# The second part of an output projection: another order of its features, two blocks interleaved, and four weight sets of the next stage prepared in it

## The chip, the cores and the metric

The kernel runs on one core of a Trainium2 chip. The metric is the device time of one execution in microseconds (us); the time of before is the median of three runs.

## The reference

One layer of a streaming encoder, for 256 new frames and 64 frames of a running stream, together 320 positions, with 2048 features:

```
h = RMSNorm(x);  p = h @ w_in
A = conformer convolution of 1024 channels (width 31, group norm, swish)
B = gated DeltaNet, 8 heads of 128
x = x + RMSNorm(concat(A, B) @ w_out)          # the output projection
h = RMSNorm(x);  gu = causal depthwise conv (width 3) of h @ w_up
x = x + RMSNorm((silu(gate) * up) @ w_down)
```

Outputs are the two results and the new states. All is float32.

## The kernel before

**Layout and arithmetic.** Activations lie with 128 features on the partitions and the 320 positions along the free dimension, so the 2048 features are 16 tiles. Every weight and every activation is split into a high part (fp32r) and a remainder, and each product is three matmuls: high by high, high by remainder, remainder by high. A weight set is loaded by SyncE's queue into a staging tile `w` (pool `wst`, three buffers, L207), ScalarE converts it to the high part `whi` (L214), and VectorE takes the remainder `wlo` (L215); both lie in pool `wsp`, three buffers each. A staging buffer is free again when its remainder is taken, a `wsp` buffer when the last matmul has read it. `load_split` does all three. `block_matmul` (L222 on) runs a whole block so and calls `tick` after every matmul, which lets background jobs (the convolution's and DeltaNet's later steps) put their instructions in at chosen points.

**The output projection** has 16 output blocks and 16 feature tiles, in the order `KORDER` (0 to 7 from the convolution, 8 to 15 from the heads). Its first part (L995 to L1000) takes the first 11 features of blocks 0 to 14, with weights `w_out1` in sets of 6 and 5 features, and copies each sum from PSUM to a tile `m[n]` (L1000). Then `while jobs` (L1001) puts out what is left of the jobs; at this point that is the last step of the convolution's channel group 7: transposes (L592), the swish `af` (L594), and the split of feature 7 into `bh` (L238) and `bl` (L239). The second part (L1037 to L1063) goes over the blocks again, with the last five features and one set `w_out2[n]` of 128 x 640 each: 15 matmuls a block (L1052 to L1054). Its PSUM tiles come from pools `ps_p` (blocks 0 and 1, then 4 and 5, and so on) and `ps_t`, two buffers each. After a block VectorE adds the sum to `m[n]` (L1060), ScalarE squares it (L1020, L1023), VectorE sums the squares (L1025), and ScalarE scales `m[n]` (L1063). Block 15 does its first part here too, as 6 and 5 features and then the five. In the same loop the residual `x1` is loaded (L1041), in 16 pieces of 160 KB, and behind blocks 4 and 8 one set each of the up projection, 128 x 1024, is loaded and split into pool `ug`, which has two buffers.

**The stage behind it** (L1064 to L1110): the norm's factor (`rstd`, `rstd_rows`, with idle matmuls that keep TensorE busy), then for each feature tile k: scale (L1084), add the residual (L1085), high part (L1089) and remainder (L1090). For odd k up to 11 the up sets 2 to 7 are loaded and split here, through the common pools. For k = 1, 3 and 5 their VectorE work is queued behind the remainder of the tile before and their ScalarE work behind the last scaling of `m`. `up_group` then runs four blocks of the up projection side by side, 12 matmuls per feature (L1108). Behind it the squares of `x1` are summed for the next norm.

**Order.** Instructions of an engine run in the order in which a scheduler puts them, by priority (`tc.high_priority`) and by when it expects them to be ready. `tc.issue_after(ins)` queues what a block of code puts on the engine of `ins` behind `ins`, and only on that engine.

Of the kernel before, what the change touches and what calls it, by code (L numbers as in the profile page):

```python
# [9 lines left out]
F32 = mybir.dt.float32  # L10
F32R = mybir.dt.float32r
AF = mybir.ActivationFunctionType
ALU = mybir.AluOpType
# [4 lines left out]
P = 128  # L18
D = 2048
KB = D // P  # L20
TP = 256
TS = 64
T = TP + TS
# [5 lines left out]
HALF = 1024  # L29
NWARM = 8  # L30
GAP = 20
PRI_J = 1500
LAG_GATE = 60
LAG_CONV = 40
# [33 lines left out]
K1 = 11  # L68
# [3 lines left out]
FIRST_V = 32  # L72
NFIRST = len(FIRST)
FW = NFIRST * P
KORDER = (0, 1, 2, 3, 4, 8, 9, 10, 11, 12, 13, 5, 6, 7, 14, 15)

S_ = 4

# [22 lines left out]
def trunk_kernel(ctx, tc, ins, outs):  # L101
    nc = tc.nc
    V, S, G, PE = nc.vector, nc.scalar, nc.gpsimd, nc.tensor
    PRI_W = 600
    boost = [0]
    PRI_E = 3000
# [19 lines left out]
    def advance(job, behind=None):  # L126
        with tc.issue_after(behind or dense[0]), tc.high_priority(offset=PRI_J):
            try:
                wait, job[2], job[3], *kind = next(job[1])
                job[0] = dense[1] + wait  # L130
                job[4] = kind
            except StopIteration:
                jobs.remove(job)
        return next(i for i in reversed(nc.cur_bb.bb.instructions) if i.engine == dense[0].engine)
# [10 lines left out]
    def newest(engine, n0):  # L145
        return next((i for i in reversed(nc.cur_bb.bb.instructions[n0:]) if i.engine == engine), None)

    def tick(mm):
        dense[0] = mm.ins
        dense[1] += 1  # L150
        if dense[1] % GAP == 0:
            g, t0, behind, due = 0, held_t[0], dense[0], []
# [25 lines left out]
    act = ctx.enter_context(tc.tile_pool(name="act", bufs=1))  # L178
# [10 lines left out]
    def pv(name, a=None, b=None):  # L189
        o, w = PAR[name]  # L190
        if a is None:
            return par[:, o:o + w]
        return par[:, o + a:o + (a + 1 if b is None else b)]
# [8 lines left out]
    def load_dma(src):  # L202
        w = wst.tile([P, HALF], F32, tag="w", name="w")
        dst = w[:, 0:src.free_size()]
        if len(src.shape) == 3:
            dst = dst.rearrange("p (a f) -> p a f", a=src.shape[1])
        nc.sync.dma_start(dst, src)  # L207
        return w

    def split_w(w, width, pool=None):  # L210
        pool = pool or wsp
        hi = pool.tile([P, HALF], F32R, tag="whi", name="whi")
        lo = pool.tile([P, HALF], F32R, tag="wlo", name="wlo")
        S.copy(hi[:, 0:width], w[:, 0:width])  # L214
        V.tensor_tensor(lo[:, 0:width], w[:, 0:width], hi[:, 0:width].bitcast(F32), ALU.subtract)  # L215
        return hi, lo

    def load_split(src, width, pool=None):
        with tc.high_priority(offset=boost[0]):
            return split_w(load_dma(src), width, pool)  # L220
# [51 lines left out]
    def keep_warm(ps, n, after=None):  # L272
        with ExitStack() as e:
            if after is not None:
                e.enter_context(tc.issue_after(after.ins))
            for _ in range(n):
                PE.matmul(ps, wz[:, 0:P], wz, start=True, stop=True)
# [16 lines left out]
    def hx(k):  # L294
        return hi_t[k], lo_t[k]
# [17 lines left out]
    with tc.tile_pool(name="xp", bufs=1) as xp:  # L313
# [25 lines left out]
        with tc.high_priority(offset=PRI_E):  # L339
            keep_warm(psw, NWARM)  # L340

            last = {}
# [42 lines left out]
        for k0 in range(0, KB, 2):  # L385
            hi, lo = pre[k0 // 2]
            for ks in ((k0,), (k0 + 1,)) if k0 < 4 else ((k0, k0 + 1),):
                for wt in (hi, lo):
                    for k in ks:
                        for i, b in enumerate(FIRST):  # L390
                            ps = ready[b][:, 0:T]
                            o = (k - k0) * FW + i * P
                            w = wt[:, o:o + P]
                            xh, xl = hx(k)
# [171 lines left out]
    def conv_tail(b, cvt, left):  # L566
        while left[0]:
            yield GAP, 0, 0
        yield LAG_CONV, 0, 1
# [80 lines left out]
    def gdn_tail(h, st, kq, vT):  # L650
        s = h % NS
        while not gate or (s and "kq" not in st) or (h // NS > 1 and "free" not in sts[h // NS - 2]):
            yield GAP, 1 + 2 * s, 1
        if s == 0:
# [72 lines left out]
    def base_inverse(bt, st):  # L727
# [9 lines left out]
        G.memset(wi_t[:, 0:256:17], 1.0)  # L737
        yield 2 * GAP, 0, 0

        d8, w8 = (t.rearrange("p (b x) -> p b x", b=2)[:, :, 0:128].rearrange("p b (r c) -> p b r c", c=16)[:, :, :, 0:8]  # L740
                  for t in (dn_t, wi_t))
        for r in range(6, -1, -1):
# [5 lines left out]
            if r in (3, 0):  # L748
                yield GAP, 0, 0
        tmp = tmp_t.rearrange("p (r c s) -> p r c s", r=8, c=8)  # L750
# [3 lines left out]
        V.tensor_reduce(x, tmp, AX.X, ALU.add)  # L754
        yield GAP, 0, 0
        V.tensor_tensor(tmp, wi[:, 0:8, 0:8].unsqueeze(2).to_broadcast((nb, 8, 8, 8)),
# [234 lines left out]
    def bx(k):  # L991
        return b_hi[KORDER[k]], b_lo[KORDER[k]]

    m = []
    for n in range(KB - 1):  # L995
        psm = ps_p.tile([P, 512], F32, tag="p", name="psm")
        block_matmul(psm[:, 0:T], ins["w_out1"][n], bx, (6, 5))
        m.append(act.tile([P, T], F32, tag=f"hl{n}", name=f"m{n}"))
        with tc.high_priority(offset=PRI_E):
            S.copy(m[n], psm[:, 0:T])  # L1000
    while jobs:  # L1001
        advance(jobs[0])
    pa.close()
    pb = ctx.enter_context(ExitStack())
    res = pb.enter_context(tc.tile_pool(name="res", bufs=1, reuse_waits="tile"))
# [10 lines left out]
    def square_acc(k, x, whole=False):  # L1016
        nonlocal acc
        if k == 0:
            acc = fb.tile([P, T], F32, tag="acc", name="acc")
            S.activation(acc, x, AF.Square)  # L1020
            return acc
        sq = fb.tile([P, T], F32, tag="sq", name="sq")
        S.activation(sq, x, AF.Square)  # L1023
        if whole or k < KB - 1:
            V.tensor_tensor(acc, acc, sq, ALU.add)  # L1025
        return sq

    ug = tc.tile_pool(name="ug", bufs=2, reuse_waits="tile")
    ugp = ug.__enter__()
    up_src = ins["w_up"][0:4].rearrange("a p f -> p a f")  # L1030

    def up_weights(kk, pool=None):
        return load_split(up_src[:, :, kk * 256:(kk + 1) * 256], HALF, pool)

    upw = []
    nk2 = KB - K1
    for n in range(KB):  # L1037
        hi, lo = load_split(ins["w_out2"][n], nk2 * P)
        if n in (4, 8):
            upw.append(up_weights(len(upw), ugp))  # L1040
        nc.sync.dma_start(x1[:, n:n + 1, :], ins["x"][:, n:n + 1, :])  # L1041
        if n == KB - 1:
            nc.sync.dma_start(fpar, ins["fpar"])
        whole = n == KB - 1
        pool = (ps_p, ps_t)[n // 2 % 2]
        psm = pool.tile([P, 512], F32, tag=pool.name[-1], name="psm2")
        if whole:
            block_matmul(psm[:, 0:T], ins["w_out1"][n], bx, (6, 5), False)
        for j in range(nk2):
            xh, xl = bx(K1 + j)  # L1050
            o = j * P
            PE.matmul(psm[:, 0:T], hi[:, o:o + P], xh, start=(j == 0 and not whole), stop=False)  # L1052
            PE.matmul(psm[:, 0:T], hi[:, o:o + P], xl, start=False, stop=False)
            PE.matmul(psm[:, 0:T], lo[:, o:o + P], xh, start=False, stop=(j == nk2 - 1))  # L1054
        with tc.high_priority(offset=PRI_E):
            if whole:
                m.append(act.tile([P, T], F32, tag=f"hl{n}", name=f"m{n}"))
                src = psm[:, 0:T]
            else:
                V.tensor_tensor(m[n], m[n], psm[:, 0:T], ALU.add)  # L1060
                src = m[n]
            last = square_acc(n, src)
            held = S.activation(m[n], src, AF.Identity, scale=pv("g2", n)).ins  # L1063
    boost[0] = 0  # L1064
    rb2 = act.tile([P, T], F32, tag="rb", name="rb2")
    hi2, lo2 = [], []
    with tc.high_priority(offset=PRI_E):
        psw = ps_p.tile([P, 512], F32, tag="p", name="psw")
        rr, mm = rstd([acc, last])
        keep_warm(psw, 5, mm)  # L1070
        rb1, mm = rstd_rows(rr)
        keep_warm(psw, 10, mm)
        split = None
        for k in range(KB):
            if k % 2 == 1 and k < 13:
                with ExitStack() as e:
                    if k < 7:
                        e.enter_context(tc.issue_after(split))
                        e.enter_context(tc.issue_after(held))
                    upw.append(up_weights(len(upw)))  # L1080
            with ExitStack() as e:
                if 0 < k < 4:
                    e.enter_context(tc.issue_after(added))
                V.tensor_tensor(m[k], m[k], rb1, ALU.mult)  # L1084
            added = V.tensor_tensor(x1[:, k, :], x1[:, k, :], m[k], ALU.add).ins  # L1085
            g = pv("g3", k)
            hi2.append(act.tile([P, T], F32R, tag=f"hh{k}", name=f"hi2_{k}"))
            lo2.append(act.tile([P, T], F32R, tag=f"hl{k}", name=f"lo2_{k}"))
            S.activation(hi2[k], x1[:, k, :], AF.Identity, scale=g)  # L1089
            split = V.scalar_tensor_tensor(lo2[k], x1[:, k, :], g, hi2[k].bitcast(F32), ALU.mult, ALU.subtract).ins  # L1090
# [98 lines left out]
    with tc.high_priority(offset=PRI_E):  # L1189
        last = square_acc(KB - 1, held_y[:, 0:T])  # L1190
# [25 lines left out]
    for step in PLAN_Y.split():  # L1216
        how, ks = step[0], step[1:]
        n = 2 if len(ks) == 4 else 1
        k = int(ks[:len(ks) // n])
# [16 lines left out]
def pack(inputs):  # L1236
# [12 lines left out]
    w_in_t = wtile(w_in[:, :6144], 48)  # L1249
    w_out = wtile(f["w_out"][0].reshape(KB, P, D)[list(KORDER)].reshape(D, D), 16)  # L1250
    par = np.concatenate([
# [63 lines left out]
```

## Time and profile before

| | |
|---|---|
| runs | 1498.56 us median of 3 (1497.97 to 1499.13) |
| profiled execution, from first to last instruction | 1497.8 us |
| PE, DVE, ACT, POOL busy | 99%, 67%, 49%, 15% |
| mean granted TensorE clock | 0.997 |
| DMA | 224.22 MB, mean 150 GB/s |
| first matmul of the second part's block 0 | 500.00 us |
| first matmul of block 15 | 535.98 us |
| first matmul of the up group | 548.88 us |

The page gives the profiled execution's own time as its span; what lies around the span isn't shown by it, and the median of the runs is 0.8 us longer. In the profile PE is TensorE's matmuls, PEld its weight loads, DVE VectorE, ACT ScalarE, POOL GpSimd and SPq the queue of SyncE, which issues the loads. A timeline row gives start and length in us, engine, line, operation, what is written from what, and the count of merged instructions; in brackets the idle time before it and what ended it. The records of successive matmuls overlap, so the distance of their starts is what one costs.

### The profile page before, as it was taken

To read this page: it belongs to the slowest core of one execution; us is meant where nothing else is said; L and a number is where in the kernel's file an instruction comes from. 1 tells how busy PE (TensorE), PEld (TensorE's weight loads), DVE (VectorE), ACT (ScalarE), POOL (GpSimd) and SP (SyncE) were. 2 spreads that over 40 slices of the span, in tenths; PEclk is the share of its full clock that TensorE was granted. 3 is DMA by queue.
4 is the path that set the end of the run, shared out by engine and by line. 5 is a ranking of instruction groups with operands and counts; after the bars stand their busy time and mean duration, and the time that the engine had idled before them with its cause. 6 is when DMAs were issued, how large, how long until landed. Compare 5 with 4: busy or idle time off the path is not lost.

```text
span 1497.8 us, 27263 instructions
## 1 busy us (share of the span) xinstructions
PE 1481.6 (99%) x10609; PEld 1460.4 (98%) x10610; DVE 996.1 (67%) x1816; ACT 727.9 (49%) x1329; POOL 229.2 (15%) x390
## 2 busy tenths in 40 slices
PE   9999999999999999999999999999999999999998
PEld 8999999989999999999999999999999999999997
DVE  6779886978989678766345666445666545666554
ACT  7764556554544565544434444334444333444453
POOL 0111101120010000332002222002223101222101
PEclk9999999999999999999999999999999999999999
DMA  8435453544434744444554444455444455444453
GB/s 289 142 128 157 141 155 120 146 139 134 130 106 142 221 151 141 148 149 128 149 169 151 151 154 134 140 156 164 154 152 141 136 146 173 153 146 152 130 152 118
DMA packets 98281, 224.22 MB, mean 150 GB/s; under 512 B 18792, under 2 KB 39528, under 8 KB 98152
## 3 DMA queue, kind: packets, MB, share of 16 engines
q1 hardware_dynamic: 98008, 222.45, 47.7%
q8 instruction: 83, 1.36, 0.4%
q14 instruction: 46, 0.38, 0.1%
q10 hardware_dynamic: 144, 0.03, 0.0%
HBM read 215.33 MB, written 7.12 MB: 149 GB/s over the span
## 4 chain that ended last, share of the span: by engine, by line
PE 86%; DVE 6%; ACT 3%; DMA 2%; issue 2%; POOL 1%; SPq 0%; ACTq 0%; DVEq 0%
PE psu L234 13%; PE psu L231 13%; PE psu L230 13%; PE psdn L230 7%; PE psdn L231 6%; PE psdn L234 6%; PE psq L234 2%; PE psq L230 2%; PE psq L231 2%; PE psm L231 2%; PE psm L230 2%; PE psm L234 2%; DVE wlo L215 1%; PE psu L1108 1%; PE ps_first L395 1%
## 5 line engine op out<-in xcount | busy, mean ns | idle before, releaser
L214 ACT CAST whi<-w 128x1024 fp32r<-128x1024 f32 (+2 forms) x440 | 412.6, 940 | 481.7 <-PE psu L231 169.0
L215 DVE TENSOR_TENSOR wlo<-w,whi 128x1024 fp32r<-128x1024 f32 (+2 forms) x440 | 477.0, 1085 | 199.0 <-ACT whi L214 127.8
L230 PE MATMUL psu<-hi,whi 128*128 128x320 f32 x1344 | 397.0, 309 | 0.0
L231 PE MATMUL psu<-lo,whi 128*128 128x320 f32 x1344 | 397.0, 309 | 0.0
L230 PEld LDWEIGHTS psu<-hi,whi 128*128 128x128 f32 x1344 | 252.3, 188 | 0.0
L231 PEld LDWEIGHTS psu<-lo,whi 128*128 128x128 f32 x1344 | 252.3, 188 | 0.0
L234 PE MATMUL psu<-hi,wlo 128*128 128x320 f32 x1344 | 224.4, 309 | 0.0
L234 PEld LDWEIGHTS psu<-hi,wlo 128*128 128x128 f32 x1344 | 204.0, 188 | 0.0
L231 PE MATMUL psdn<-gl,whi 128*128 128x320 f32 x660 | 195.9, 310 | 0.0
L1141 POOL COPY nffn<-fbuf 128x2 f32<-128x2 f32 x88 | 101.5, 1153 | 586.9 <-DVE fbuf L1139 583.7
L1139 DVE TENSOR_TENSOR fbuf<-psu,rb 128x256 f32<-128x256 f32 x88 | 37.3, 424 | 168.9 <-PE psu L234 168.9
L230 PE MATMUL psdn<-gh,whi 128*128 128x320 f32 x480 | 142.8, 309 | 0.0
L231 PEld LDWEIGHTS psdn<-gl,whi 128*128 128x128 f32 x660 | 123.9, 188 | 0.3
L230 PE MATMUL psq<-hh,whi 128*128 128x320 f32 x352 | 106.2, 315 | 0.0
L231 PE MATMUL psq<-hl,whi 128*128 128x320 f32 x352 | 104.1, 309 | 0.0
L230 PEld LDWEIGHTS psdn<-gh,whi 128*128 128x128 f32 x480 | 90.1, 188 | 0.0
L234 PE MATMUL psdn<-gh,wlo 128*128 128x320 f32 x480 | 89.9, 309 | 0.0
L234 PEld LDWEIGHTS psdn<-gh,wlo 128*128 128x128 f32 x480 | 75.3, 188 | 0.0
L230 PEld LDWEIGHTS psq<-hh,whi 128*128 128x128 f32 x352 | 66.1, 188 | 0.3
L231 PEld LDWEIGHTS psq<-hl,whi 128*128 128x128 f32 x352 | 66.1, 188 | 0.2
L560 DVE SCALAR_TENSOR_TENSOR cvt<-ub,par,cvt 128x320 f32<-128x320 f32 x120 | 65.2, 543 | 0.2
L1184 DVE TENSOR_TENSOR y<-y,psdn 128x320 f32<-128x320 f32 x45 | 22.0, 488 | 59.1 <-PE psdn L234 59.1
(356 smaller groups left out, 2483.3 us busy)
## 6 DMA issues: line engine op xcount, KB each, us to landing
w<-in_w_up SPq DMA_DIRECT2D x176, 512.0 KB, 3.6
w<-in_w_in SPq DMA_DIRECT2D x88, 512.0 KB, 3.9
w<-in_w_down SPq DMA_DIRECT2D x64, 384.0 KB, 3.1
w<-in_w_down SPq DMA_DIRECT2D x64, 320.0 KB, 3.0
w<-in_w_out SPq DMA_DIRECT2D x32, 320.0 KB, 3.8
w<-in_w_out SPq DMA_DIRECT2D x16, 384.0 KB, 3.2
w<-in_w_first SPq DMA_DIRECT2D x6, 512.0 KB, 6.9
wtp<-wsp SPq DMA_DIRECT2D x4, 640.0 KB, 6.0
```

What stands on the lines that cost most here:

```text
L214: S.copy(hi[:, 0:width], w[:, 0:width])
L215: V.tensor_tensor(lo[:, 0:width], w[:, 0:width], hi[:, 0:width].bitcast(F32), ALU.subtract)
L230: tick(PE.matmul(ps, wh, xh, start=(first and k0 + j == 0), stop=False))
L231: tick(PE.matmul(ps, wh, xl, start=False, stop=False))
L234: tick(PE.matmul(ps, lo[:, j * P:(j + 1) * P], xh, start=False, stop=(final and k0 + j == nk - 1)))
L395: tick(PE.matmul(ps, w, xh, start=(k == 0 and wt is hi), stop=(k == KB - 1 and wt is lo)))
L560: return lambda: V.scalar_tensor_tensor(acc, x, w, acc, ALU.mult, ALU.add)
L1108: PE.matmul(pss[i][:, 0:T], wt[:, o:o + P], x, start=(k == 0 and n == 0), stop=(k == KB - 1 and n == 2))
L1139: V.tensor_tensor(buf[:, 2:258], psu[:, 0:TP], rb2[:, 0:TP], ALU.mult)
L1141: G.tensor_copy(nffn[:, b, 0, :], buf[:, 256:258])
L1184: V.tensor_tensor(y[:, n, :], y[:, n, :], psd[:, 0:T], ALU.add)
```

## The change

- `KORDER` ends in 5, 14, 15, 6, 7 where it ended in 5, 6, 7, 14, 15. The weights are packed by the same order.
- Block 0 of the second part does its first four features, then block 1 does its first four, then block 0 its last one (feature 7) and block 1 its last one. Both are evacuated after that.
- The split of block 2's weights is traced under `issue_after(flush)`, where `flush` is ScalarE's last instruction of the jobs that were left: its conversion stands behind the cast of feature 7.
- Pool `ug` has four buffers, and up sets are loaded and split behind blocks 4, 6, 8 and 10; the later loop does so only for k = 5, 7, 9 and 11.

```
-KORDER = (0, 1, 2, 3, 4, 8, 9, 10, 11, 12, 13, 5, 6, 7, 14, 15)
+KORDER = (0, 1, 2, 3, 4, 8, 9, 10, 11, 12, 13, 5, 14, 15, 6, 7)
...
+    flush = len(nc.cur_bb.bb.instructions)
     while jobs:
         advance(jobs[0])
+    flush = newest(mybir.EngineType.Activation, flush)
...
-    ug = tc.tile_pool(name="ug", bufs=2, reuse_waits="tile")
+    ug = tc.tile_pool(name="ug", bufs=UGB, reuse_waits="tile")
...
+    def second(n, psm, w, js):
+        hi, lo = w
+        for j in js:
+            xh, xl = bx(K1 + j)
+            o = j * P
+            PE.matmul(psm, hi[:, o:o + P], xh, start=(j == 0 and n < KB - 1), stop=False)
+            PE.matmul(psm, hi[:, o:o + P], xl, start=False, stop=False)
+            PE.matmul(psm, lo[:, o:o + P], xh, start=False, stop=(j == nk2 - 1))
...
     for n in range(KB):
-        hi, lo = load_split(ins["w_out2"][n], nk2 * P)
-        if n in (4, 8):
+        with ExitStack() as e:
+            if n == 2:
+                e.enter_context(tc.issue_after(flush))
+            w2 = load_split(ins["w_out2"][n], nk2 * P)
+        if n in (4, 6, 8, 10):
             upw.append(up_weights(len(upw), ugp))
...
+        if n == 0:
+            opened[0] = psm, w2
+            second(n, psm[:, 0:T], w2, range(nk2 - 1))
+            continue
+        if n == 1:
+            second(n, psm[:, 0:T], w2, range(nk2 - 1))
+            second(0, opened[0][0][:, 0:T], opened[0][1], (nk2 - 1,))
+            second(n, psm[:, 0:T], w2, (nk2 - 1,))
+        else:
+            second(n, psm[:, 0:T], w2, range(nk2))
+        for n, psm in ((0, opened[0][0]), (1, psm)) if n == 1 else ((n, psm),):
+            evacuate(n, psm, whole)
...
-            if k % 2 == 1 and k < 13:
+            if k % 2 == 1 and 4 < k < 13:
```

The body of `evacuate` is the old code behind the block's matmuls, unchanged.

More of the change, by code (lines that the diff above doesn't have):

```diff
@@ L31 @@
 GAP = 20
+UGB = 4
 PRI_J = 1500
@@ L1036, in trunk_kernel, with evacuate @@
     nk2 = KB - K1
-    for n in range(KB):
-        hi, lo = load_split(ins["w_out2"][n], nk2 * P)
-        if n in (4, 8):
+    def second(n, psm, w, js):
[6 more added lines that the diff above has]
+            PE.matmul(psm, lo[:, o:o + P], xh, start=False, stop=(j == nk2 - 1))
+    last = held = None
+    def evacuate(n, psm, whole):
+        nonlocal last, held
+        with tc.high_priority(offset=PRI_E):
+            if whole:
+                m.append(act.tile([P, T], F32, tag=f"hl{n}", name=f"m{n}"))
+                src = psm[:, 0:T]
+            else:
+                V.tensor_tensor(m[n], m[n], psm[:, 0:T], ALU.add)
+                src = m[n]
+            last = square_acc(n, src)
+            held = S.activation(m[n], src, AF.Identity, scale=pv("g2", n)).ins
+    opened = {}
+    for n in range(KB):
+        with ExitStack() as e:
[3 more added lines that the diff above has]
+        if n in (4, 6, 8, 10):
             upw.append(up_weights(len(upw), ugp))
@@ L1048, in trunk_kernel @@
             block_matmul(psm[:, 0:T], ins["w_out1"][n], bx, (6, 5), False)
[L1049 to L1063, printed above, removed]
+        if n == 0:
[6 more added lines that the diff above has]
+            second(n, psm[:, 0:T], w2, (nk2 - 1,))
+        else:
+            second(n, psm[:, 0:T], w2, range(nk2))
+        for n, psm in ((0, opened[0][0]), (1, psm)) if n == 1 else ((n, psm),):
+            evacuate(n, psm, whole)
     boost[0] = 0
```

## The prediction

> **What bounds the kernel now.** I read the page first, then the busy time by stretches, then the chain that ended last, then the timelines of PE, ACT, DVE and of the load queue between 495 and 600 us, where the changed lines run.
>
> ```profile
> span 1497.8 us, 27263 instructions
> PE 86%; DVE 6%; ACT 3%; DMA 2%; issue 2%; POOL 1%; SPq 0%; ACTq 0%; DVEq 0%
> ```
>
> TensorE carries 86% of the chain, and most of that is work that the change doesn't touch. So the most the change can do is to remove the few us in which PE stands still near its lines, and the most it can lose is what it makes PE stand still anew. Here is how busy the engines are there (columns: stretch, length, then PE, weight loads, DVE, ACT and POOL in us with instruction counts, granted clock, DMA share, GB/s):
>
> ```profile
> 503.00:525.00 22.00, 21.14 (x142) 20.80 (x143) 15.43 (x26) 15.25 (x27) 0.00 (x0) 1.00 0.86 271
> 549.00:579.00 30.00, 29.72 (x196) 28.47 (x195) 29.34 (x56) 15.14 (x25) 0.00 (x0) 1.00 0.38 124
> ```
>
> Two stages, two limits. In the first (the projection's second part) the DMA engines are 86% busy and DVE and ACT have a third free. In the second (residual, new activations, first up group) DVE is full: 29.34 of 30 us. The chain through the first stage, in order of time (start, us, what):
>
> ```profile
> 496.95 4.13 DMA w<-in_w_out
> ...
> 502.79 3.50 DMA w<-in_w_up
> ...
> 508.65 4.43 DMA w<-in_w_out
> ...
> 516.35 4.13 DMA w<-in_w_out
> ...
> 522.97 0.41 PE psm L1054
> ```
>
> The chain runs not along PE but along the weight supply: a set is loaded into one of three staging buffers, converted by ACT, its remainder taken by DVE, and only then is the buffer free for the third set after it. It is PE's turn only at 522.97. PE's own stops there:
>
> ```profile
> 499.76 0.49 PE L592 MATMUL pt_c<-cst,un 128*128 128x128 f32 x3
> 500.00 0.39 PE L1052 MATMUL psm<-bh,whi 128*128 128x320 f32 x1
> ...
> 502.28 0.42 PE L1052 MATMUL psm<-bh,whi 128*128 128x320 f32 x1 [1.15 <-ACT m L1000]
> ...
> 503.30 0.56 PE L1052 MATMUL psm<-bh,whi 128*128 128x320 f32 x2 [0.31 <-ACT bh L238]
> ...
> 506.56 0.31 PE L1052 MATMUL psm<-bh,whi 128*128 128x320 f32 x1
> ...
> 522.97 0.41 PE L1054 MATMUL psm<-bh,wlo 128*128 128x320 f32 x1 [0.56 <-DVE wlo L215]
> ...
> 535.98 0.31 PE L230 MATMUL psm<-bh,whi 128*128 128x320 f32 x1
> ```
>
> Blocks 2 to 14 take from 506.56 to 535.98, 29.42 us with some 0.7 us lost at 522.97, so a block of 15 matmuls is 28.7 / 13 = 2.2 us. Blocks 0 and 1 should take 4.4 us from 500.00 and end at 504.4; they end at 506.56. So **2.16 us** are lost at the front, and 0.7 at block 9.
>
> **The front: order, interleaving, the queued conversion.** Why the front stalls is seen on ACT, and on DVE's last row:
>
> ```profile
> 501.18 0.72 ACT L214 CAST whi<-w 128x640 fp32r<-128x640 f32 x1 [3.53 <-DMA w<-in_w_out]
> 501.81 0.42 ACT L1000 COPY m<-psm 128x320 f32<-128x320 f32 x1
> 502.13 0.63 ACT L594 ACTIVATE af<-pt_c,par 128x320 f32<-128x320 f32 x1
> 502.79 0.46 ACT L238 CAST bh<-af 128x320 fp32r<-128x320 f32 x1
> ...
> 505.14 0.73 ACT L214 CAST whi<-w 128x640 fp32r<-128x640 f32 x1 [1.90 <-PE psm L1053]
> ...
> 506.31 1.05 ACT L214 CAST whi<-w 128x1024 fp32r<-128x1024 f32 x1
> ```
>
> ```profile
> 503.28 0.49 DVE L239 TENSOR_TENSOR bl<-af,bh 128x320 fp32r<-128x320 f32 x1 [0.52 <-ACT bh L238]
> ```
>
> ACT stood 3.53 us on block 2's weights, with three things queued behind it that were ready at 500.0 to 500.25: the copy of m14 (block 1's PSUM waits for it, 1.15 us) and the two steps that make feature 7, the last of the convolution. Feature 7's parts came at 503.25 and 503.77, while the order asked for it third.
>
> After the change the conversion of block 2 stands behind feature 7's cast. The copy runs at about 500.1, then 0.63 and 0.46 us of ACT and 0.49 us of DVE: feature 7 is there by 502.1. Features 14 and 15 move ahead of 6 and 7, and blocks 0 and 1 both do four features (24 matmuls, 3.5 us) before either needs feature 7, at 503.5. That is a margin of 1.4 us, and the PE front loss should go whole: blocks 0 and 1 end at 504.4. The interleaving adds no instruction. It holds block 0's weights until its last hi matmul, 500.00 + 26 x 0.147 = 503.8, where before the next conversion waited for them until 505.14; so block 3's conversion comes 1.3 us sooner, and block 5's load, which takes its staging buffer, is issued at about 505.5. The price: block 2's conversion moves from 501.18 to about 501.5, and the first up set's load, which takes that buffer, from 502.79 to 503.1, some 0.3 us. Queued behind the conversion on ACT is then only block 3's, which can't start before 503.8, so nobody else waits for it.
>
> **The two further up sets.** The loads go through one queue in program order. Up sets stand now behind the loads of blocks 4, 6, 8 and 10, not 4 and 8: up 1 is moved past the loads of blocks 7 and 8, up 2 and up 3 (until now behind all of these) past those of 9 to 15 and the two sets of block 15's first part. Their conversions (1.05 us of ACT each, as the last ACT row above, and 1.2 us of DVE, as the 1.21 us row below) fit into the third that is free: about 2.3 us more on engines that have 6.6 to spare in 503 to 525. What they use up is turns of the staging buffers:
>
> ```profile
> 506.76 0.33 SPq L207 DMA_DIRECT2D w<-in_w_out  x1
> ...
> 521.34 0.33 SPq L207 DMA_DIRECT2D w<-in_w_out  x1
> ...
> 530.90 0.33 SPq L207 DMA_DIRECT2D w<-in_w_out  x1
> 532.48 0.33 SPq L207 DMA_DIRECT2D w<-in_w_out  x1
> ```
>
> ```profile
> w<-in_w_out SPq DMA_DIRECT2D x12, 320.0 KB, 4.0
> ...
> w<-in_w_up SPq DMA_DIRECT2D x1, 512.0 KB, 4.2
> w<-in_w_out SPq DMA_DIRECT2D x1, 384.0 KB
> ```
>
> The first fence has issues of block 5 (506.76), block 11 (521.34) and the two sets of block 15's first part (the 384 KB one at 530.90). The second counts the sets issued from 506.76 on: 14. From block 5's issue to the 384 KB one are 12 steps in 24.14 us, **2.01 us a set**. PE eats a set per 2.2 us, so supply gains only 0.2 us a block and each extra up set puts it back by 2. With two more sets it is 14 steps: 505.5 + 28.2 = 533.7. Its conversion started 3.36 us after its issue:
>
> ```profile
> 534.26 0.82 ACT L214 CAST whi<-w 128x768 fp32r<-128x768 f32 x1
> ```
>
> So block 15's first weights are there at 533.7 + 3.4 + 0.8 = 537.9, where PE, freed of its front loss, wants them at 504.4 + 13 x 2.2 = 533.0, and where before it took them at 535.98. The front's gain is eaten and **+1.9 us** more; I expect it as waits at blocks 7, 9, 11 and 15, some 1 to 1.6 us each. Bounds: blocks 11 on, without residual loads in the queue and without an up set, ran at 11.14 / 6 = 1.86 us a set, which gives 531.5, ready 535.7: -0.3 us. The stretch 506.76 to 521.34, one up set in seven steps, ran at 2.08: 534.6, ready 538.8: +2.8. The mean is taken, because the new stretch has both kinds.
>
> **The stage after the norm.** The up group's matmuls and DVE (start, us):
>
> ```profile
> 549.84 0.75 PE L1108 MATMUL psu<-hi,wlo 128*128 128x320 f32 x4
> ...
> 571.59 0.85 PE L1108 MATMUL psu<-hi,whi 128*128 128x320 f32 x4
> ...
> 573.60 0.75 PE L1108 MATMUL psu<-hi,whi 128*128 128x320 f32 x4
> ```
>
> ```profile
> 557.15 1.21 DVE L215 TENSOR_TENSOR wlo<-w,whi 128x1024 fp32r<-128x1024 f32 x1
> 558.29 0.54 DVE L1090 SCALAR_TENSOR_TENSOR lo<-x,par,hi 128x320 fp32r<-128x320 f32 x1
> ```
>
> From 549.84 to 571.59 stand 35 groups of four matmuls, 35 x 0.587 = 20.5 us of work in 21.75; 0.1 more goes by 573.60. So PE loses **1.3 us** to DVE, which is full here. A remainder keeps it for 1.14 us (the step from 557.15 to 558.29). With up 2 and up 3 done beforehand DVE has 2.3 us less, which is more than PE loses: next late is PE itself, so the 1.3 us go. Bounds: 0.6 if the later sets still bunch up, 1.3 at most. What leaves ACT here costs nothing now:
>
> ```profile
> 544.77 2.94 ACT L214 CAST whi<-w 128x1024 fp32r<-128x1024 f32 x3
> 548.16 0.56 ACT L1089 ACTIVATE hi<-x,par 128x320 fp32r<-128x320 f32 x1 [0.45 <-DVE x L1085]
> ```
>
> The three conversions run while the norm is made, and the first activation after them still waits 0.45 us for DVE. One risk: the sets of k = 7 and 9 are not tied behind the last scaling and could stand on ACT ahead of the last square, 0 to 1.05 us (one conversion). I take 0, since the later sets ran behind it in this trace, and keep 1.05 in the range. A last piece:
>
> ```profile
> 591.59 0.83 PE L256 MATMUL pst<-cst,acc 128*128 128x1 f32 x6 [0.23 <-DVE acc L1025]
> ```
>
> The sum of squares comes 0.2 us late behind the same DVE queue: -0.2.
>
> **Sum.** +1.9 - 1.3 - 0.2 = +0.4 us against the span of 1497.8. The median of the runs, 1498.56, lies 0.8 above that span, and takes the same difference: 1498.9.
>
> **The skill against the sum.** The rows give 271 GB/s at a DMA share of 0.86, so about 315 GB/s when all engines are busy. The Trainium skill ("DMA: Bandwidth & Descriptors", Specifications) puts the limit of memory for one core at about 358 GB/s. By that figure the two sets' 1.05 MB would cost an estimated 2.9 us where transfers, not buffers, set the pace, against 4.0 us by my count of turns (two steps of 2.01); the sum would then come out near -0.7 us instead of +0.4. The rows stay the basis.
>
> **Rivals.** *Supply keeps pace.* If the sets flow at less than the 1.86 us a set of the undisturbed end, because three buffers are refilled sooner when ACT is no longer held up, PE never waits: 2.16 + 0.7 + 1.3 + 0.2 = 4.4 us gone, 1494.2. For it: block 5's set starts 1.3 us sooner. Against it: no stretch of the trace ran faster than 1.86, and this one has four up sets in it.
>
> *Transfers saturate (slower).* Between 503 and 525 the queue also brings the residual, and two 512 KB sets are put into that same stretch: 1.05 MB / 315 GB/s = 3.3 us more in 22 us of which 3.1 are idle. If the engines can't fill those gaps, every landing gets later and a step grows by 3.3 / 14 = 0.24 us to 2.25: 505.5 + 31.5 = 537.0, ready 541.2, +5.2 - 1.5 = +3.7 us, 1502.3. It decides once the DMA share there passes about 0.95. For it: the share of 0.86. Against it: the step is mostly buffer turns, whose ACT and DVE parts don't grow.
>
> *The front doesn't change.* If the order on ACT still leaves the copy or feature 7 behind a load, block 5's load stays at 506.76 and the sum is 1.3 higher: 1500.2.
>
> **How the numbers follow.** Forecast 0.62, supply keeps pace 0.19, transfers saturate 0.14, front unchanged 0.05. 0.2% is 3 us, about what a measurement of this kernel can tell from no change. The forecast's own range is 1496.8 (the -0.3 bound with the whole later gain of 1.5) to 1500.8 (+2.8 with a later gain of only 0.6), and 1501.8 with the late square. Beyond -3 us lies only the first rival: faster 0.19. Beyond +3 lie the saturated case and a sliver of the forecast with the late square: slower 0.16. Same: 0.65. The range reaches down to the first rival's 1494.2, a little below it, and up to the late square, 1494.0 to 1501.8; it leaves out the saturated case and the far ends, under 0.2 together.
>
> **What would show it.** Right: no wait of PE between 500 and 504.4; block 3's conversion near 503.8; waits of PE on conversions or remainders at blocks 7, 9, 11, and block 15 starting near 537.9; then an up group without the waits between 560 and 573. Wrong: block 15 starting before 535 (supply wasn't the limit), or the DMA share above 0.95 with landings over 5 us, or ACT's last square delayed by a conversion.

## The result, and the profile after

The changed kernel takes 1501.01 us, the median of 12 runs (1499.33 to 1502.47), against 1498.32 us of 12 runs of the kernel before beside it (1496.31 to 1499.36). The ratio is 1.0018, its 95% interval 1.0010 to 1.0027. So the change costs 2.7 us. That is inside 0.2% and inside the range, but it is no zero, and the forecast had +0.4.

The profiled execution of after took 1499.90 us. Here are its span and the shares of its chain by engine, from the page:

```profile
span 1498.1 us, 27264 instructions
PE 82%; DVE 7%; ACT 4%; DMA 3%; issue 2%; POOL 2%; SPq 0%; ACTq 0%; DVEq 0%
```

The span is only 0.3 us above the 1497.8 of before, though the medians are 2.7 apart. Every run on record took 1.7 to 1.9 us more than its own span, not the 0.8 by which the median of before lies above the span of its profile. So the profiled execution of before was a slow one (an estimate: 1497.8 + 1.8 = 1499.6 us, against a median of 1498.32), and that of after a fast one (1499.90 against 1501.01). The difference lies ahead of the changed lines. Block 0's first matmul came at 500.00 in the profile of before and at 497.78 here; over the profiles of this study it lies between 496.7 and 500.0 (one kernel that changed the work ahead of it left out), even where nothing ahead of it was edited. So I don't compare clock times. I compare two stretches, each from its own start: the **second part**, from block 0's first matmul to the start of block 15's last matmul, and the **up group**, from its first matmul to the second norm's broadcast. What lies between them took 5.20 us in both kernels. First PE's rows of after (start, us; in brackets the idle time and what ended it):

```profile
497.78 0.39 PE L1046 MATMUL psm<-bh,whi 128*128 128x320 f32 x1
...
502.27 0.31 PE L1046 MATMUL psm<-bh,whi 128*128 128x320 f32 x1
...
509.88 0.41 PE L1048 MATMUL psm<-bh,wlo 128*128 128x320 f32 x1 [0.30 <-DVE wlo L216]
...
514.82 0.41 PE L1046 MATMUL psm<-bh,whi 128*128 128x320 f32 x1 [0.57 <-ACT whi L215]
...
515.68 0.42 PE L1048 MATMUL psm<-bh,wlo 128*128 128x320 f32 x1 [0.30 <-DVE wlo L216]
...
521.05 0.41 PE L1046 MATMUL psm<-bh,whi 128*128 128x320 f32 x1 [1.00 <-ACT whi L215]
...
522.38 0.41 PE L1046 MATMUL psm<-bh,whi 128*128 128x320 f32 x1 [0.77 <-ACT whi L215]
...
527.75 0.42 PE L1046 MATMUL psm<-bh,whi 128*128 128x320 f32 x1 [1.00 <-ACT whi L215]
528.83 0.42 PE L1046 MATMUL psm<-bh,whi 128*128 128x320 f32 x1 [0.52 <-ACT whi L215]
...
537.87 0.31 PE L231 MATMUL psm<-bh,whi 128*128 128x320 f32 x1
...
545.75 0.31 PE L1048 MATMUL psm<-bh,wlo 128*128 128x320 f32 x1
```

And the row of before that answers to the last one:

```profile
543.68 0.31 PE L1054 MATMUL psm<-bp,wlo 128*128 128x320 f32 x1
```

Blocks 0 and 1 now take 4.49 us without a wait; the front stall is gone. Counted at 15 matmuls a block, the new waits are for the sets of block 5 (509.88), block 7 (514.82 and 515.68), blocks 9 and 10 (521.05, 522.38) and blocks 11 and 12 (527.75, 528.83); the set after an up set is late each time, and PE falls further behind at each. From 530 on PE waits for no weights, at block 15 neither. The second part takes 545.75 - 497.78 = 47.97 us against 543.68 - 500.00 = 43.68 of before: **+4.3 us**.

The busy times of the two stretches whose rows the prediction shows (the same columns):

```profile
503.00:525.00 22.00, 19.05 (x122) 17.49 (x121) 16.27 (x27) 15.38 (x28) 0.88 (x4) 1.00 0.91 297
...
549.00:579.00 30.00, 30.00 (x201) 28.70 (x199) 28.77 (x57) 14.17 (x26) 0.00 (x0) 1.00 0.26 88
```

In the first PE falls from 21.14 to 19.05 of 22 us, and the DMA share rises from 0.86 to 0.91. In the second PE has no gap any more (29.72 before). The up group, rows of before and then of after:

```profile
548.88 1.12 PE L1108 MATMUL psu<-hi,whi 128*128 128x320 f32 x4
...
593.98 0.49 PE L269 MATMUL psb<-cst,rr 128*128 128x128 f32 x3
```

```profile
550.95 1.12 PE L1136 MATMUL psu<-hi,whi 128*128 128x320 f32 x4
...
594.22 0.49 PE L270 MATMUL psb<-cst,rr 128*128 128x128 f32 x3
```

45.10 us become 43.27: **-1.8 us**. Together +2.5 us, close to the measured +2.7. Now the chain of after through the second part (start, us, what):

```profile
503.72 4.45 DMA w<-in_w_out
508.24 0.73 ACT whi L215
...
509.85 4.11 DMA w<-in_w_out
...
521.21 4.44 DMA w<-in_w_up
525.67 1.06 ACT whi L215
526.75 1.24 DVE wlo L216
528.00 2.83 DMA w<-in_w_out
...
532.52 3.72 DMA w<-in_w_out
536.32 0.85 ACT whi L215
```

It is the same kind of chain as before, load, conversion, remainder and the next load into the freed buffer, and one of the four up sets stands in it in full: 521.21 to 528.00, 6.8 us for one turn of one buffer. The loads of up sets 1 to 3 (counted from 0), in SyncE's queue:

```profile
508.01 0.38 SPq L208 DMA_DIRECT2D w<-in_w_up  x1
...
514.10 0.38 SPq L208 DMA_DIRECT2D w<-in_w_up  x1
...
521.21 0.38 SPq L208 DMA_DIRECT2D w<-in_w_up  x1
```

They are 6.1 and 7.1 us apart, with two blocks' sets (4.4 us of PE's work) between them.

### The profile page after: what moved, and what is told of

Read it like the earlier page. It is cut to its first block, busy times and chain, and to the rows that moved or that the text cites. A ratio compares the mean times of both kernels' runs of the same rounds, so it can differ in the third digit from the quotient of the medians.

```text
span 1498.1 us, 27264 instructions
## 1 busy us (share of the span) xinstructions
PE 1480.8 (99%) x10610; PEld 1459.3 (97%) x10610; DVE 996.3 (67%) x1816; ACT 727.0 (49%) x1329; POOL 228.7 (15%) x390
## 4 chain that ended last, share of the span: by engine, by line
PE 82%; DVE 7%; ACT 4%; DMA 3%; issue 2%; POOL 2%; SPq 0%; ACTq 0%; DVEq 0%
PE psu L231 13%; PE psu L232 13%; PE psu L235 13%; PE psdn L231 7%; PE psdn L232 6%; PE psdn L235 6%; DVE wlo L216 2%; PE psu L1136 2%; PE psq L231 2%; PE psq L232 1%; PE psq L235 1%; PE psm L235 1%; PE psm L231 1%; PE psm L232 1%; PE ps_first L396 1%
## 5 line engine op out<-in xcount | busy, mean ns | idle before, releaser
L561 DVE SCALAR_TENSOR_TENSOR odd<-ub,par,odd 128x320 f32<-128x320 f32 x112 | 60.9, 544 | 0.3
```

The lines of the kernel that those rows point to most:

```text
L561: return lambda: V.scalar_tensor_tensor(acc, x, w, acc, ALU.mult, ALU.add)
```

## The experiments

Theory A: the further up sets take turns of the three shared staging buffers, and the turns are the cost. B: the transfers saturate. C: the conversions lengthen ScalarE's line. Every run, compared in the two stretches of its own profile (us; sum: both against before's 43.68 and 45.10):

| kernel | second part | up group | sum | measured against before |
|---|---|---|---|---|
| after | 47.97 | 43.27 | +2.5 | +2.7 |
| after, a second profile | 48.47 | 43.27 | +3.0 | +2.7 (one run) |
| front alone | 43.03 | 45.09 | -0.7 | -1.1 |
| four sets alone | 51.05 | 43.28 | +5.6 | +4.9 |
| residual loads late | 44.98 | 43.27 | -0.5 | -1.0 (one run) |
| own staging, free to move | 40.79 | 43.27 | -4.7 | +1.0 |
| own staging, held in place | 42.83 | 43.27 | -2.7 | -3.5 |
| two sets late | 43.39 | 43.27 | -2.1 | -2.6 |
| three sets late | 41.88 | 43.68 | -3.2 | -4.4 |
| order and interleaving alone | 44.99 | 45.10 | +1.3 | -0.1 (one run) |
| queued conversion alone | 43.44 | 45.10 | -0.2 | -1.0 (one run) |
| three late, all sets in own staging | 40.79 | 56.70 | +8.7 | +8.0 |
| three late, the first in own staging | 40.78 | 43.58 | -4.4 | -5.2 |

But for the kernel with own staging that is free to move, which lost time ahead of these stretches, sums and times agree within 1.4 us. So the stages hold the effects that are larger than that. All sums rest on one profile of before; the +1.3 and -0.2 of the front's two parts are too small to be told from nothing by one run each.

**The front alone.** The changed kernel with two up sets, as before:

```
-UGB = 4
+UGB = 2
...
-        if n in (4, 6, 8, 10):
+        if n in (4, 8):
...
-            if k % 2 == 1 and 4 < k < 13:
+            if k % 2 == 1 and k < 13:
```

> The front alone: order of features, interleaving and queued conversion as changed; up sets as before (two, behind blocks 4 and 8). Theory A (the three staging buffers set the pace; each further up set takes a turn of them): blocks 0 and 1 run without a wait, block 5's load comes over 1 us sooner, nothing is added, so the second part is 1.3 to 2.9 us shorter and the stage after the norm unchanged: 1.3 to 2.9 us faster than before. Theory B (transfers saturate): the same sign, since no byte is added, but smaller, under 1 us, as earlier residual loads crowd the weights. Theory C (the up sets' conversions stand in ACT's line ahead of the next blocks' conversions and of late squares): as A.

1496.88 against 1497.94 us, ratio 0.9990 (0.9981 to 0.9999). The front stall is gone, yet only 1.1 of its 2.2 us is kept:

```profile
519.58 0.42 PE L1048 MATMUL psm<-bh,wlo 128*128 128x320 f32 x1 [0.95 <-DVE wlo L216]
```

PE now comes to block 9 sooner, and waits there longer than in before (0.95 instead of 0.56), with 0.23 more at block 5. With two up sets the supply already binds. The 1.1 us lie between what the theories expected (A and C 1.3 or more, B under 1), so this run doesn't choose between them. It is the nearest kernel to set the two further up sets against: the second part takes 43.03 us with two and 47.97 with four, so a further set costs 2.5 us.

**The four sets alone**, on the kernel before:

```
-    ug = tc.tile_pool(name="ug", bufs=2, reuse_waits="tile")
+    ug = tc.tile_pool(name="ug", bufs=4, reuse_waits="tile")
...
-        if n in (4, 8):
+        if n in (4, 6, 8, 10):
...
-            if k % 2 == 1 and k < 13:
+            if k % 2 == 1 and 4 < k < 13:
```

> The four up sets alone: loaded and split behind blocks 4, 6, 8 and 10, with the old order, no interleaving and no queued conversion. Theory A: two turns of 2 us more, less about 1 us that block 15's first set had to spare, less 1.5 us after the norm: 1 to 2.5 us slower than before. Theory B: as slow or slower, 2 to 4 us, with the DMA share between blocks 2 and 12 above 0.95. Theory C: 1 to 3 us slower, with waits of ACT on an up set and PE waiting right behind them.

1502.86 against 1497.94 us, ratio 1.0032 (1.0021 to 1.0043). That is more than any theory expected (4 us at most). The second part grows by 7.4 us, the up group gains its 1.8. Some of the loss is TensorE's clock, which fell here (windows of this kernel; the column after POOL is the granted clock):

```profile
526.00:531.00 5.00, 2.68 (x15) 1.92 (x13) 2.82 (x5) 3.64 (x7) 0.00 (x0) 1.00 0.36 109
531.00:536.00 5.00, 4.83 (x23) 4.81 (x23) 3.41 (x7) 2.70 (x5) 0.00 (x0) 0.66 0.72 217
```

From 531.45 to 535.19 us 15 matmuls took 3.74 us, where 15 take 2.2 elsewhere: about 1.5 us. The 3.4 that remain would fit B's 2 to 4, but the DMA share between 503 and 525 us was 0.91, not above 0.95. This run doesn't choose either.

**Residual loads late.** The changed kernel with its 16 residual loads behind block 15's weights:

```
-        nc.sync.dma_start(x1[:, n:n + 1, :], ins["x"][:, n:n + 1, :])
...
             block_matmul(psm[:, 0:T], ins["w_out1"][n], bx, (6, 5), False)
+            with tc.issue_after(newest(mybir.EngineType.SP, n0)):
+                for i in range(KB):
+                    nc.sync.dma_start(x1[:, i:i + 1, :], ins["x"][:, i:i + 1, :])
```

> The changed kernel with the residual's 16 loads moved behind block 15's weights, so that 2.6 MB leave the stretch; read from block 0's first to block 15's last matmul (the stage behind may wait for the residual). Theory A: landings get shorter by the queue's share, a turn falls from about 6.2 to some 5.2 us: 43 to 45 us. Theory B: all waits go, 41 to 42 us. Theory C: little change, 46 to 48 us.

One run of 1497.84 us against 1498.85. Between 503 and 525 us the DMA share falls to 0.67, and still 2.4 us of waits stand at blocks 9 to 11, so a queue that is a third idle doesn't end them. But the second part is 3 us shorter than the changed kernel's, and the loads land sooner: in that stretch the median from issue to landing is 2.9 us for a block's set and 3.4 for an up set, where the changed kernel has 4.4 for both. So the residual's traffic does lengthen a turn. A holds; B is not the whole of it, and not nothing.

**Own staging, free to move.** The up sets' loads go to two buffers of their own, so they take no turn of the shared ones:

```
-    def load_dma(src):
-        w = wst.tile([P, HALF], F32, tag="w", name="w")
+    def load_dma(src, own=None):
+        w = wst.tile([P, HALF], F32, tag="w", name="w") if own is None else own.tile([P, HALF], F32, tag="uw", bufs=2, name="uw")
...
-            return split_w(load_dma(src), width, pool)
+            return split_w(load_dma(src, pool), width, pool)
```

> The changed kernel, but the four up sets are loaded into two staging buffers of their own, so that they take no turn of the three others; bytes, conversions and their places in the program stay. Theory A: the waits at the later blocks go; second part 2 to 3 us shorter than before and the stage after the norm 1.5: 3 to 4.4 us faster than before. Theory B: as the changed kernel, 2 to 3 us slower than before, since the bytes are the same. Theory C: between, 1 us either side of before, with PE's waits left where ACT does an up conversion.

1498.92 against 1497.94 us, ratio 1.0006 (0.9997 to 1.0015), a miss as a test. With nothing to wait for, the scheduler put the sets' work into the end of the first part, ahead of the convolution's last taps, and PE waited there for VectorE (waits of this kernel from 460 to 500 us; us in total, times, longest):

```profile
PE pt_c L576 <- DVE cvt L555: 3.5, 1, 3.5
```

What it did show is the second part without any wait: 40.79 us, the floor for all that follows.

**Own staging, held in place.** The same, with each up set's load, conversion and remainder queued behind those of its block:

```
+            ends = [newest(t, n0) for t in (mybir.EngineType.SP, mybir.EngineType.Activation, mybir.EngineType.DVE)]
+            with ExitStack() as e:
+                for i in ends:
+                    e.enter_context(tc.issue_after(i))
+                upw.append(up_weights(len(upw), ugp))
```

> As the run with own staging, but each up set's load, conversion and remainder are now also held behind those of the block it follows (4, 6, 8 or 10), since in that run the scheduler had moved all four into the end of the first part. Same bytes and same places as in the changed kernel; only the turns of the three staging buffers are saved. Theory A (turns): from block 0's first to block 15's last matmul 41 to 43 us, as with the up sets out of the way, and 2.5 to 4 us faster than before. Theory B (transfers): 46 us or more, still 2 us slower than before. Theory C (conversions in ACT's line): 44 to 46 us, PE's waits right behind up conversions, about as fast as before.

1495.32 against 1498.85 us, ratio 0.9975 (0.9966 to 0.9984): 3.5 us faster than before, with the same four sets behind the same blocks. Its window and its two waits:

```profile
503.00:525.00 22.00, 20.89 (x141) 20.36 (x139) 18.62 (x31) 18.72 (x33) 0.00 (x0) 1.00 0.93 302
```

```profile
515.59 0.42 PE L1048 MATMUL psm<-bh,wlo 128*128 128x320 f32 x1 [0.77 <-DVE wlo L216]
...
525.37 0.42 PE L1048 MATMUL psm<-bh,wlo 128*128 128x320 f32 x1 [0.71 <-DVE wlo L216]
```

The engines move more (302 GB/s at 0.93) than in the changed kernel (297 at 0.91), and 5.1 of its 48.0 us are gone. So the transfers had room, and the turns were the main cost; B is refuted as the main cause. One more thing differs here: the hold fixes the place of an up set's conversion in ScalarE's line, while in the changed kernel up set 2 stood behind a square that waited for block 8's sum (ACT of the changed kernel):

```profile
518.41 0.47 ACT L1026 ACTIVATE sq<-m 128x320 f32<-128x320 f32 x1 [1.23 <-DVE m L1059]
518.87 1.05 ACT L215 CAST whi<-w 128x1024 fp32r<-128x1024 f32 x1
```

That conversion came 4.77 us after its load's issue (514.10), against 4.46 for up set 3 (521.21 to 525.67), which only waited for its load. So an estimate of what the order cost there is 0.3 us; a run that changes the order alone is missing. C is left for the 2.0 us above the floor: both waits are for remainders, on engines that are now busy 18.6 and 18.7 of 22 us. I made no run that changes the conversions alone, so C's share is open.

**Two and three sets late.** The sets stay in the shared buffers, but two (or three) of them are loaded behind block 15's sets, their conversions behind the last scaling and the last sum of squares:

```
-        if n in (4, 6, 8, 10):
+        if n in (4, 8):
             upw.append(up_weights(len(upw), ugp))
...
             block_matmul(psm[:, 0:T], ins["w_out1"][n], bx, (6, 5), False)
+            with tc.issue_after(held), tc.issue_after(summed):
+                for _ in range(2):
+                    upw.append(up_weights(len(upw), ugp))
```

For three sets late the first condition is `if n == 4:` and the range 3.

> The changed kernel with up sets behind blocks 4 and 8 as before, and the third and fourth loaded behind block 15's sets and converted behind block 14's scaling and sum, while PE works through block 15 and ACT and DVE stand idle. Theories A, B and C agree on the sign here: the front's gain of 1.3 to 2.9 us as in the run of the front alone, plus the 1.5 us after the norm: 2.8 to 4.4 us faster than before. If the conversions run into block 15's last square, up to 1 us less.

> One up set in the loop, behind block 4; the second, third and fourth behind block 15's sets. Theories A and C: block 9's wait, which two up sets in the loop leave, shrinks by up to a turn: 3 to 4.5 us faster than before, up to 1.5 faster than with two late. If the third late conversion delays the last square, no better than with two late. Theory B: as with two late.

Two late: 1495.32 against 1497.94 us, ratio 0.9981 (0.9972 to 0.9990). Three late: 1494.49 against 1498.85, ratio 0.9970 (0.9958 to 0.9982). With two late the gain of 2.6 us is a little under the 2.8 to 4.4 that were expected, with three it is inside 3 to 4.5. The second part takes 43.39 and 41.88 us, and the up group keeps its gain (43.27 and 43.68). Each set that leaves blocks 5 to 12 gives 1.5 to 2.3 us: 47.97, 43.39 and 41.88 with four, two and one there.

**The changed kernel once more**, to see whether it now and then shows the clock drop of the four sets alone:

> The changed kernel once more, for a second profile: whether its waits stand at the same blocks, and whether the granted clock falls after them, as it did to 0.50 for 3.6 us in the run of the up sets alone, after PE had been busy 2.7 of 5 us. If it falls in some executions of the changed kernel, they are 1.5 to 2 us longer than the others, which would go some way to explain why the median lies above the first profiled execution.

1501.52 us, a miss: the granted clock stayed at 1.00, and the same waits stand at the same blocks. What differs is the start of block 0, at 499.00 and not 497.78. So the small span of the first profile was an earlier front, not a faster second part.

**The front's parts.** The order and the interleaving without the queued conversion (the kernel of the front alone, with two up sets), and the queued conversion alone on the kernel before:

```
-            if n == 2:
-                e.enter_context(tc.issue_after(flush))
             w2 = load_split(ins["w_out2"][n], nk2 * P)
```

```
+    flush = len(nc.cur_bb.bb.instructions)
     while jobs:
         advance(jobs[0])
+    flush = newest(mybir.EngineType.Activation, flush)
...
-        hi, lo = load_split(ins["w_out2"][n], nk2 * P)
+        with ExitStack() as e:
+            if n == 2:
+                e.enter_context(tc.issue_after(flush))
+            hi, lo = load_split(ins["w_out2"][n], nk2 * P)
```

> The front alone (other order of features, blocks 0 and 1 interleaved, two up sets) without the queued conversion. If the front's stall of the kernel before came from block 2's weight conversion standing ahead of the last copy of m on ScalarE, the copy and the split of feature 7 are late again by about 1.1 us: the first two blocks take 4.4 us plus 0.5 to 1.2 us, and the second part from the first matmul to block 15 is near 43 to 44 us. If the order of features and the interleaving alone remove the stall (rival), the first two blocks take 4.4 us and the second part is 43.0 as in the run of the whole front.

> The kernel before with the queued conversion alone. If the conversion ahead of the copy was the front's stall, at least 1.1 us of block 0's and 1's stall of 2.2 us goes, and what is left is the wait for features 5 to 7 in the old order (up to 1 us). The second part's length falls by little (43.68 to 42.7 to 43.7), since the later blocks then wait for the weights, as in the run of the whole front. Rival: with features 5 to 7 still in the middle of the block, the stall stays above 2 us.

One run each, 1497.63 and 1496.72 us against 1497.69. Both expectations were half wrong: either part alone takes the whole stall of blocks 0 and 1 away, but without the queued conversion a wait of the same size comes back at block 3. With the queued conversion alone, in the old order, PE has no wait before block 9; ScalarE's line is (the queued conversion is the last row):

```profile
497.31 0.43 ACT L1000 COPY m<-psm 128x320 f32<-128x320 f32 x1 [2.22 <-PE psm L234]
...
498.30 0.46 ACT L238 CAST bh<-af 128x320 fp32r<-128x320 f32 x1
498.66 0.73 ACT L214 CAST whi<-w 128x640 fp32r<-128x640 f32 x1
```

With order and interleaving alone the copy and feature 7 still stand behind a conversion, but they are asked for later, and the first two blocks don't wait. The next wait comes from ScalarE's order, in which up set 0 stands ahead of block 3's conversion and waits 3.00 us for its load. ACT, then PE:

```profile
502.55 1.05 ACT L215 CAST whi<-w 128x1024 fp32r<-128x1024 f32 x1 [3.00 <-DMA w<-in_w_up]
...
505.14 1.34 ACT L215 CAST whi<-w 128x640 fp32r<-128x640 f32 x2
```

```profile
505.90 0.41 PE L1046 MATMUL psm<-bh,whi 128*128 128x320 f32 x1 [2.21 <-ACT whi L215]
```

**Three late, all four sets in own staging.** The kernel with three late sets, its loads as in own staging held in place:

> One up set behind block 4, three behind block 15's sets, as in the run with three late ones, and the up sets in two staging buffers of their own. Buffer turns: no wait for weights is left in the second part but at most one of 0.4 us, its length is 41 to 42 us (41.88 with three late sets, 40.79 without any wait), and the run is 4 to 5 us faster than before. Transfers saturate: no better than the run with three late sets in the shared buffers, 41.9 us or more. Conversions on ScalarE: the late sets' conversions run during the second norm, so nothing changes against the run with three late sets.

1505.67 against 1497.69 us, ratio 1.0064 (1.0050 to 1.0078), the worst of all. The second part has no wait left (40.79 us), but the last set's load was issued only at 533.94, when the remainder of the first late set had freed one of the two own buffers. Its conversion ran at 542.57, amid the stage behind the second part, and VectorE was given its remainder behind most of that stage's steps. DVE, then PE, then windows of this kernel:

```profile
564.46 1.22 DVE L216 TENSOR_TENSOR wlo<-uw,whi 128x1024 fp32r<-128x1024 f32 x1
```

```profile
565.73 1.44 PE L1147 MATMUL psu<-hi,wlo 128*128 128x320 f32 x4 [11.23 <-DVE wlo L216]
```

```profile
555.00:559.00 4.00, 0.00 (x0) 0.00 (x0) 4.00 (x9) 1.35 (x3) 0.00 (x0) 1.00 0.38 135
559.00:560.00 1.00, 0.00 (x0) 0.00 (x0) 1.00 (x4) 0.67 (x2) 0.00 (x0) 0.90 0.14 53
560.00:565.00 5.00, 0.00 (x0) 0.00 (x0) 5.00 (x12) 2.00 (x4) 0.00 (x0) 0.50 0.00 0
...
569.00:570.00 1.00, 1.00 (x6) 1.00 (x5) 0.90 (x2) 0.83 (x2) 0.00 (x0) 0.50 0.00 0
570.00:571.00 1.00, 1.00 (x9) 1.00 (x7) 0.79 (x3) 0.79 (x2) 0.00 (x0) 0.98 0.00 0
```

PE stands 11.23 us behind a remainder of 1.2 us, and then works at half the clock for its first 4 us. All three theories expected some 4 us of gain: none of them looked at the order in which VectorE gets a late set's remainder.

**Three late, the first in own staging.** Only the set behind block 4 has a buffer of its own and is held in place; the three late ones go through the shared buffers:

```
+        w = wst.tile([P, HALF], F32, tag="w", name="w") if own is None else own.tile([P, HALF], F32, tag="uw", bufs=1, name="uw")
...
+        return load_split(up_src[:, :, kk * 256:(kk + 1) * 256], HALF, pool, None if kk else pool)
```

> As the run with one up set behind block 4 and three late ones, which go through the shared buffers again; only the set behind block 4 has a staging buffer of its own. Buffer turns: the wait of 0.37 us for block 5's weights goes, the second part is 41.2 to 41.9 us, and the run is 4 to 5 us faster than before. If own staging as such, and not the place of one late remainder, was what made the run with own staging for all four slow: a wait of several us in the second norm's up group again, slower than before.

1492.54 us (6 runs, 1492.27 to 1493.64) against 1497.72, ratio 0.9967 (0.9955 to 0.9979): 5.2 us faster than before, and the fastest kernel here. Its window and the ends of its second part:

```profile
503.00:525.00 22.00, 22.00 (x152) 22.00 (x151) 17.55 (x33) 17.96 (x34) 1.23 (x4) 1.00 0.81 267
```

```profile
497.11 0.39 PE L1046 MATMUL psm<-bh,whi 128*128 128x320 f32 x1
...
537.89 0.31 PE L1048 MATMUL psm<-bh,wlo 128*128 128x320 f32 x1
```

PE is busy for all 22 us, and the second part is at its floor, 40.78 us, a little below the 41.2 to 41.9 expected. The remainders of the three late sets started at 532.95, 534.45 and 537.35, before the norm began. So own staging of the first set does no harm. In the run before this one the harm was the place of one remainder, and its late load came of three late sets in two own buffers.

## Why the prediction was right in its mechanism and short in its sum

**The front: right.** No PE wait until block 5, and block 3's conversion at 501.88, 4.1 us after block 0's start (3.8 forecast). But the three were not needed together. The queued conversion alone leaves no wait before block 9; the order and the interleaving alone free blocks 0 and 1, and then 2.21 us are lost at block 3. And what the whole front gives is 1.1 us, since the supply takes back the rest.

**The supply: the failed step.** The prediction took 2.01 us a set in 14 steps, put the 384 KB set's issue 33.7 us after block 0's start (500.00 there) and block 15's start at 37.9. The pace was right: 14 steps from 503.72 to 532.52 are 28.8 us, 2.06 a set. From block 0's start, the chain began 0.4 us later than forecast (5.9 for 5.5), the steps took 0.6 more, and landing and conversion 4.6 instead of 4.2: the set was ready at 536.32 + 0.84 - 497.78 = 39.4 us, 1.5 later than 37.9. That is 0.6 beyond the upper bound (38.8). Moreover block 15 did not start when its set was ready, but at 40.1 us: PE was still behind from the waits for blocks 11 and 12. The prediction read the finish of a chain of sets at its last set; the wait that decides is at the set that is latest against PE's own need, and behind up set 3 PE has four more blocks (11 to 14) at 2.2 us ahead of block 15 that no faster supply can shorten. So +1.9 was forecast for block 15 and 40.1 - 36.0 = +4.1 measured: of the 2.2 us between, the three small terms make about 1.5 and the earlier waits 0.7. The waits stood at blocks 5, 7, 9 to 12, not at 7, 9, 11 and 15. The bounds had varied the pace alone, not the chain's start or the landing, so they were too narrow; and the stretch behind the lower one was not free of residual loads, as one was issued in it (at 523.36). In the profile of after block 15 starts at 537.87, the very time that was forecast, by chance: block 0 had started 2.2 us earlier.

**The stage after the norm: right, a little small.** -1.5 forecast, -1.8 measured; the up group takes the same 43.27 or 43.28 us in six other profiles of the table, and 43.58 to 43.68 where three sets come late and no remainder is misplaced. The late square was not seen: the up group's start keeps its 5.20 us behind block 15.

**The sum.** +4.3 and -1.8 give +2.5 where the text had +1.9 and -1.5. The median of the measured runs lies 2.7 above that of before: inside the range and inside 0.2%, by a step that was undersized, not by the balance that was forecast.

**The rivals.** *Supply keeps pace* fell with the waits for weights. *Transfers saturate* named the right sign and nearly the size of the second part (+5.2 there), but by a mechanism that the runs refute: the share was 0.91, not 0.95, and with own staging more bytes per us flowed with fewer waits. *The front doesn't change* fell at the front. The sentence that weighed the Trainium skill's 358 GB/s ("DMA: Bandwidth & Descriptors", Specifications) gave -0.7; the measured +2.7 lies on the other side of the turns' count, so the count of turns was the better basis.

## What to carry to other kernels

Where a chain of loads, conversions and releases through a few shared buffers feeds PE at barely PE's own pace, an extra set costs at least a step of that chain (2.06 us a set here, and 2.5 us for each of the two further sets), not its conversions alone; so put it behind the last set that PE needs soon, or give it a buffer of its own. Forecast such a chain set by set against the time at which PE wants each set, and take the latest, which need not be the last. And when work is given a place of its own, look at where each engine's queue then puts its last step: one remainder at the wrong end of VectorE's line cost 11 us.

## What the runs showed of the hardware that was not expected

TensorE's clock fell to half. In the kernel with three late sets and own staging for all, PE was idle from 554.50 to 565.73 us; the granted clock was still 1.00 from 555 to 559 us, 0.90 in the next microsecond, and 0.50 until 570 us, four microseconds after PE had work again. The Trainium skill ("TensorE: Matmul & The Clock Gate", Why this matters for your kernels) advises against gaps of PE of more than about 3 us between bursts of matmuls, and this run agrees. The kernel with the four sets alone does not fit it so simply: its longest gap was under 2 us (from the matmul at 527.27 to 529.38), yet after a stretch with PE busy for 2.68 of 5 us the clock was 0.50 from 532 to 535 us, and a matmul took 0.27 instead of 0.147 us. The busy share doesn't sort the runs either. In the second profile of the changed kernel PE was busy for less of a stretch, and the clock stayed at 1.00 there and behind it:

```profile
519.00:524.00 5.00, 2.63 (x17) 2.11 (x15) 3.15 (x5) 3.47 (x6) 0.00 (x0) 1.00 0.89 289
```

With order and interleaving alone one gap was longer (2.21 us), and the clock stayed as well. So the fall cost the four sets alone about 1.5 us, and what sets it off below 3 us of idle time isn't shown by these runs.
